# Hybrid decoder trunk: heads' sums and meta part behind the queries, groups' gate and row squares behind bank copies

## The chip, the cores and the metric

The kernel runs on one core of a Trainium2 chip, as one program. The metric is the device time of one execution in microseconds (us). A core has five engines, each with an instruction queue of its own that it works off in order: PE (TensorE, matrix products, which land in PSUM banks), DVE (VectorE), ACT (ScalarE), POOL (GpSimd) and SP (SyncE, which here only issues DMAs). They wait for one another through semaphores. An instruction that waits holds up everything behind it in its own queue.

## The reference

One layer of a decoder: four groups of a short gated convolution and four heads of retention (linear attention with decay) run side by side on the same normalised input, one projection goes in and one out, and a normalisation ends it. Sixteen learned "meta" rows precede the 2048 rows of the sequence.

```python
def reference(x, meta, norm1_g, w_in, conv_w, ret_norm_g, w_out, final_g):
    h = jnp.concatenate([meta_b, x], axis=1)          # 16 + 2048 rows of 1024
    hn = rms_norm(h, norm_g)
    cx, cb, cc, cg, q, k, v, rg = jnp.split(hn @ w_in, 8, axis=-1)   # 8 x 512
    conv_out = cb * conv3(cc * cx, conv_w) * silu(cg)  # causal, 3 taps, per channel
    qf, kf = rotary(q) * 128**-0.5, rotary(k)          # 4 heads of 128
    ret = head_group_norm(retention_chunkwise(qf, kf, v))   # chunks of 128, running state
    mixed = jnp.concatenate([conv_out, ret * silu(rg)], axis=-1)
    h = h + mixed @ w_out
    return rms_norm(h, final_g)[:, N_META:]
```

## The kernel before

**Rounds and units.** The sequence is worked in two rounds (`r`) of 1024 columns. A round has eight units: units 0 to 3 are heads, 4 to 7 convolution groups. `UNITS` gives their order: 4, 0, 1, 2, 3, 5, 6, 7 in the first round and 0 to 7 in the second. In the first round unit 4 is worked by `group_plain`, all other groups by `conv_group`, the heads by `head`. The output projection follows (`output`).

**Quads.** A unit makes two products of 256 x 1024 weights with 1024 x 1024 activations. Each is a `quad`: a Strassen-Winograd scheme of seven block products, numbered 0 to 6 here, into three PSUM banks. Every float32 factor is split in a high and a low part, rounded to fp32r (`split`: ACT writes the high part, DVE the low one), and one block product is 12 matmuls of 128 x 512: four slices times low-by-high, high-by-low, high-by-high. A head's first quad makes keys and values, its second queries and gate; a group's first quad makes the two factors of the convolution's input, its second gate and outer factor.

**Between the products.** `quad` has ACT copy a bank after products 0, 2 and 3 (`copy`, tile `tc`), because later products add into the same bank: product 2 needs the copy after 0, product 4 the one after 2, product 5 the one after 3. After products 0 and 2 it takes a step of a caller's list (`step`; its ACT instructions are kept behind the copy). `take(i, j, ...)` is called with a finished block, after products 1, 4, 5 and 6; mostly DVE reads the bank and the copy there.

**Weights.** `stationary` loads four raw blocks (`ra`), has POOL make four sums of them (`sa` and, in place, `ra`) and splits seven matrices into `wh` (ACT, line 104) and `wl` (DVE, line 116), with three buffers each. They are used in the order of the products; the fourth comes from `sa`.

**Sums.** The Winograd scheme needs four sums of the activations' blocks too. For the second round and for the output they are made ahead: `prepare` is a generator; each `next(later, None)` loads four blocks (`x` or `w`), forms four sums on DVE (lines 177 and 116, with one ACT scaling at line 180 for `x`) and stores them in DRAM (`sums_x`, `sums_w`). `MAKES_SUMS` names the units that take one such step each, at their end.

**Meta.** In the first round each unit multiplies the 16 meta rows by its first weights (`meta_products`, line 412, while the unit before it ends). `meta_state` then loads a rotary table (`mr`), adds and rotates on 16 partitions of DVE (tile `mk`; lines 423 to 437), lets PE form the head's first state (line 439) and ACT copy it. `meta_carry` does the like for a group.

**Row factors.** `row_factors` is a generator for the root mean square of the rows of the next round. Eight steps load 128 rows each and let ACT square and add them (`row_squares`, two instructions on `n` and their accumulator reads); for each half of the round `spread_factors` forms the factors (DVE, POOL's power at line 293) and `spread` puts them on all partitions (DVE line 300, PE line 307, ACT lines 310 and 312).

**Order of the work.** A scheduler lists the instructions of each engine from the order in which the code states them and its own idea of times. `tc.issue_after(i)` keeps the instructions of a block that go to the engine of `i` behind `i`; those for other engines it leaves free.

Of the kernel before, what the change touches and what calls it, by code (L numbers as in the profile page):

```python
# [8 lines left out]
F32 = mybir.dt.float32  # L9
# [4 lines left out]
ALU = mybir.AluOpType  # L14
# [23 lines left out]

MAKES_SUMS = (0, 1, 2, 5), (0, 1, 2, 4)

# [33 lines left out]
def hybrid_trunk(ctx: ExitStack, tc: tile.TileContext, t, out: bass.AP, chunk_decay):  # L74
# [132 lines left out]

    copied = [None]

    def quad(w, m, take, steps=()):  # L210
# [35 lines left out]
        product(3, zb, True)  # L246
        c = copy(zb)
        product(4, xb, False)
        take(1, 1, xb, c)
# [109 lines left out]
    def row_factors(r, f):  # L359

        f.extend([row_tile("rr", r), row_tile("rr2", r), []])
        for j in range(2):
            ss = small.tile([P, 2, CH], F32, name="ss", tag="ss")
            for c in range(CH):
                row_squares(ss, r, j, c)
                yield
            f[2].append(spread_factors(ss, *(a[:, j * HB : (j + 1) * HB] for a in f[:2])))
        yield

# [56 lines left out]

    def meta_state(h, scratch):

        rot = sb.tile([P, HB], F32, name="mr", tag="tc", bufs=COPIES)[:NMETA, : 2 * P].rearrange("p (a c) -> p a c", a=2)
        nc.sync.dma_start(rot, t["rot_m"][h])  # L430
        k, v, a, b = meta_sums(scratch)
# [97 lines left out]

    def conv_group(g, r, m, f, blocks, ahead):  # L530

# [20 lines left out]
        blocks, meta = blocks  # L552
        quad(stationary(blocks), m, take)
        catch_up(0)
        if meta:
            meta_carry(g, meta)
        carry(u, g, r)
        cs = [taps(u[j], g) for j in range(2)]

        def take(i, j, pp, c):  # L560
            if i == 0:
                add(nc.vector, c, pp, c)
                mul(nc.vector, c, c, rr[j])
                nc.scalar.activation(c, c, AF.Silu)  # L564
                mul(nc.gpsimd, cs[j], cs[j], rr[j])
                mul(nc.gpsimd, cs[j], cs[j], c)
                return
            if c is not None:
                add(nc.vector, c, pp, c)
                pp = c  # L570
            mul(nc.vector, cs[j], pp, cs[j])

        n = 2 * (NG + g) + 1
        quad(stationary(load_raw(w_loads(n))), m, take)
        catch_up(1)
# [46 lines left out]

    def head(h, r, m, rot_t, f, turning, blocks, ahead, first=(), between=()):


        between = iter(between)
        to_cross = []
        k, v, late = [None, None], [None, None], []
        tables = [rot_t[:, :, j * HB : (j + 1) * HB] for j in range(2)]

# [28 lines left out]
        def take(i, j, pp, c):  # L659
            d = gen("qg")[:, :HB]  # L660
            if i == 0:
                if c is None:
                    nc.scalar.copy(out=d, in_=pp)
                else:
                    add(nc.vector, d, pp, c)
                rotary(d, tables[j])
                q[j] = d
            else:
# [20 lines left out]
        with tc.issue_after(copied[0].ins):  # L689
            join(1)  # L690
        next(between, lambda: None)()
        if blocks[1]:
            meta_state(h, blocks[1])
        blocks = ahead()
# [159 lines left out]
    for r in range(NR):  # L854
# [43 lines left out]
        else:  # L898
# [6 lines left out]
            later = prepare(load_w_out, sums_w)  # L905
        steps = row_factors(r + 1, factors[r + 1]) if r < NR - 1 else iter(())
        units = UNITS[r]
        turning = None
        special = (first, between)
        for n, unit in enumerate(units):  # L910
# [5 lines left out]
            elif unit < NG:  # L916
                if turning is None:
                    turning = [row_tile(name, 1 - r) for name in ("apart", "across")]
                blocks = head(unit, r, m, rot_t, f, turning, blocks, rest, *(special if unit == 0 else ()))
# [12 lines left out]
            if unit in MAKES_SUMS[r]:  # L932
                next(later, None)

# [43 lines left out]
```

## Time and profile before

| | |
|---|---|
| median of 3 runs | 885.62 us (884.61 to 886.62) |
| profiled execution | 885.25 us, its span 883.4 us |
| granted TensorE clock | 1.00 |
| PE busy | 866.2 us, 98% of the span |
| DVE, ACT, POOL busy | 715.5, 472.1, 397.8 us |

The page's share of busy time says that PE is hardly ever idle, but matmuls are pipelined, and a matmul counts as busy for 0.39 us while one starts every 0.23 us. Idle time of PE between two matmuls is therefore some 0.16 us less than what the second one starts late. Of the stages, which are read from the times of their instructions:

| us of the span | stage | PE idle, us |
|---|---|---|
| 62 to 122 | end of unit 4, unit 0 | 3.8 |
| 122 to 170 | unit 1 | 0.0 |
| 170 to 218 | unit 2, first products of unit 3 | 0.9 |
| 218 to 268 | unit 3 | 0.0 |
| 268 to 302 | unit 5 | 2.0 |
| 302 to 412 | units 6, 7, start of the second round | 0.0 |
| 412 to 566 | heads of the second round | 0.0 |
| 566 to 612 | unit 4 of the second round | 0.9 |
| 612 to 870 | units 5 to 7, output | 0.2 |

Each number of the last column is the length of the window less PE's busy time in it.

### The profile page before, as it was taken

The numbers are of one execution on the slowest core, as the hardware profiler recorded it, in microseconds if no ns is written. First come the engines' busy times: TensorE is split into PE (matmuls) and PEld (weight loads), VectorE is DVE, ScalarE is ACT, GpSimd is POOL, SyncE is SP. The second block draws the span as 40 slices with busy tenths as digits, with TensorE's granted clock in tenths as the row PEclk, the third lists the DMA queues.
The fourth block names the chain that finished last, engine by engine and source line by source line (L and its number), as shares of the span: only waits on it lengthen the run. The fifth ranks groups of instructions, "written<-read, shape, count | busy, mean of one in ns | idle before, by whom it ended". The sixth has DMA issues, their size and how long they took to land.

```text
span 883.4 us, 12729 instructions
## 1 busy us (share of the span) xinstructions
PE 866.2 (98%) x4279; PEld 711.1 (80%) x4279; DVE 715.5 (81%) x1176; ACT 472.1 (53%) x871; POOL 397.8 (45%) x291
## 2 busy tenths in 40 slices
PE   8999899999999999999999999999999999999996
PEld 5778787878888777888888888887888888788885
DVE  6888898979877866899989898787768699666764
ACT  8665437364655564746464645534334475545553
POOL 0554232314135554452233323254547455777873
PEclk9999999999999999999999999999999999999999
DMA  9713444343435552846345353346121493545432
GB/s 340 238 61 73 121 108 132 108 128 123 103 109 186 153 155 71 281 137 187 123 101 162 87 165 84 119 132 191 61 72 60 143 369 108 180 156 190 155 122 81
DMA packets 110033, 125.31 MB, mean 142 GB/s; under 512 B 41424, under 2 KB 58128, under 8 KB 109968
## 3 DMA queue, kind: packets, MB, share of 16 engines
q1 hardware_dynamic: 109968, 124.50, 45.6%
q8 instruction: 34, 0.56, 0.3%
q14 instruction: 31, 0.25, 0.1%
HBM read 90.92 MB, written 25.17 MB: 131 GB/s over the span
## 4 chain that ended last, share of the span: by engine, by line
PE 78%; DVE 11%; DMA 4%; issue 2%; ACT 2%; POOL 1%; SPq 1%; POOLq 0%; DVEq 0%; ACTq 0%
PE pj L221 64%; PE pj L277 7%; DVE wl L116 2%; PE ms L732 2%; PE ms L733 2%; PE ms L722 1%; DVE ml L116 1%; DMA w<-in_w_out 1%; PE ms L709 1%; DVE rot L588 1%; DMA mr<-in_rot_m 1%; DVE rot L587 1%; PE ms L412 1%; PE ms L700 1%; DVE x L177 1%
## 5 line engine op out<-in xcount | busy, mean ns | idle before, releaser
L221 PE MATMUL pj<-mh,wl 128*128 128x512 f32 x1008 | 398.5, 395 | 4.7 <-DVE wl L116 2.1
L221 PE MATMUL pj<-mh,wh 128*128 128x512 f32 x1008 | 393.1, 390 | 0.0
L221 PE MATMUL pj<-ml,wh 128*128 128x512 f32 x1008 | 392.9, 390 | 0.0
L104 ACT CAST wh<-ra 128x512 fp32r<-128x512 f32 x216 | 133.6, 619 | 257.4 <-PE pj L221 218.2
L221 PEld LDWEIGHTS pj<-mh,wl 128*128 128x128 f32 x1008 | 189.3, 188 | 48.6 <-ACT tc L228 3.6
L221 PEld LDWEIGHTS pj<-mh,wh 128*128 128x128 f32 x1008 | 189.2, 188 | 39.8
L221 PEld LDWEIGHTS pj<-ml,wh 128*128 128x128 f32 x1008 | 189.4, 188 | 38.1 <-issue 0.5
L116 DVE TENSOR_TENSOR wl<-ra,wh 128x512 fp32r<-128x512 f32 x216 | 184.6, 856 | 42.4 <-ACT wh L104 42.0
L116 POOL TENSOR_TENSOR ra<-ra 128x512 f32<-128x512 f32 x72 | 113.8, 1580 | 93.7 <-PE ms L412 58.1
L116 POOL TENSOR_TENSOR ra<-sa,ra 128x512 f32<-128x512 f32 x36 | 52.5, 1459 | 99.5 <-DVE wl L116 97.8
L113 POOL TENSOR_TENSOR sa<-ra 128x512 f32<-128x512 f32 x36 | 53.8, 1493 | 92.1 <-DMA ra<-in_w_in 32.4
L228 ACT COPY tc<-pj 128x512 f32<-128x512 f32 x108 | 62.5, 579 | 0.0
L277 PE MATMUL pj<-ml,mh 128*128 128x512 f32 x128 | 50.2, 393 | 0.1
L277 PE MATMUL pj<-mh,mh 128*128 128x512 f32 x128 | 49.9, 392 | 0.0
L277 PE MATMUL pj<-mh,ml 128*128 128x512 f32 x128 | 48.9, 399 | 0.1
L745 POOL TENSOR_TENSOR rp<-rs,neg_half 128x4 f32<-128x4 f32 x16 | 17.8, 1112 | 54.2 <-DVE rs L113 54.1
L537 POOL TENSOR_TENSOR c<-c,rr 128x512 f32<-128x512 f32 x14 | 27.6, 1968 | 24.3 <-DVE c L537 13.0
L795 DVE TENSOR_TENSOR yo<-pj,yo 128x512 f32<-128x512 f32 x32 | 21.9, 686 | 18.7 <-POOL yo L113 13.4
L797 ACT ACTIVATE rot<-yo 128x512 f32<-128x512 f32 x32 | 20.2, 630 | 31.1 <-DVE yo L795 30.7
L537 POOL TENSOR_TENSOR c<-c,tc 128x512 f32<-128x512 f32 x14 | 26.7, 1905 | 19.6 <-ACT tc L564 19.6
L800 POOL TENSOR_TENSOR z<-yo,final_g 128x512 f32<-128x512 f32 x16 | 26.9, 1681 | 16.5 <-DVE yo L795 16.5
L104 ACT CAST wh<-sa 128x512 fp32r<-128x512 f32 x36 | 22.1, 615 | 21.1 <-PE pj L221 21.0
(138 smaller groups left out, 1189.1 us busy)
## 6 DMA issues: line engine op xcount, KB each, us to landing
ra<-in_w_in SPq DMA_DIRECT2D x128, 256.0 KB, 2.8
x<-in_xT SPq DMA_DIRECT2D x48, 256.0 KB, 4.5
w<-in_w_out SPq DMA_DIRECT2D x32, 256.0 KB, 4.7
ra<-mixed SPq DMA_DIRECT2D x32, 256.0 KB, 3.0
yo<-in_x SPq DMA_DIRECT2D x32, 256.0 KB, 4.6
ra<-in_x SPq DMA_DIRECT2D x16, 256.0 KB, 3.2
mixed<-c SPq DMA_DIRECT2D x16, 256.0 KB, 2.7
sums_x<-x SPq DMA_DIRECT2D x16, 256.0 KB, 3.0
```

The lines of the kernel that those rows point to most:

```text
L104: nc.scalar.copy(out=hi, in_=src)
L113: eng.tensor_tensor(out=out, in0=a, in1=b, op=ALU.add)
L116: eng.tensor_tensor(out=out, in0=a, in1=b, op=ALU.subtract)
L221: nc.tensor.matmul(bank, a[:, ks], b, start=first and kt == 0 and n == 0, stop=kt == KH - 1 and n == 2, skip_group_check=not first,)
L228: copied[0] = nc.scalar.copy(out=c, in_=bank)
L277: nc.tensor.matmul(banks[i], a[:, ks], b, start=half + kt + n == 0, stop=half == 1 and kt == KH - 1 and n == 2,)
L537: eng.tensor_tensor(out=out, in0=a, in1=b, op=ALU.mult)
L732: nc.tensor.matmul(o[:, cs], pm[:, cs], vt[j][:, cs], start=True, stop=False)
L745: nc.gpsimd.tensor_tensor(out=rp, in0=rs, in1=neg_half.rearrange("p (c a) -> p c a", a=1), op=ALU.pow)
L795: last[0] = nc.vector.tensor_tensor(out=y, in0=pp, in1=y, op=ALU.add)
L797: nc.scalar.activation(junk, y, AF.Square, accum_out=ss[:, i, j : j + 1])
L800: nc.gpsimd.tensor_tensor(out=ys[i][j], in0=y, in1=final_g[:, j * HB : (j + 1) * HB], op=ALU.mult)
```

## The change

Four things are moved; no arithmetic is added or removed.

- **Heads' sums.** The units that take a step of `prepare` are 1, 2, 3, 5 and 1, 2, 3, 4 in the rounds, where they were 0, 1, 2, 5 and 0, 1, 2, 4. A head takes it right after its second quad, with DVE's part behind the rotation of the first half of the queries; a group with DVE's part behind its last multiplication.
- **Heads' meta part.** The table `mr` has a buffer of its own and is loaded at the head's start. All of the meta part's DVE work stands behind the rotation of the first queries.
- **Groups' gate.** The gate function of the first half (ACT's Silu, POOL's two multiplications) is stated after the copy behind product 2, not inside `take`. `quad` takes a third step, after the copy behind product 3.
- **Row squares.** The ten steps of `row_factors` (eight squares, two spreads) go one by one behind bank copies of units 6 and 7, five in each, where they were taken four at a time after units 5, 6 and 7.

```diff
-MAKES_SUMS = (0, 1, 2, 5), (0, 1, 2, 4)
+MAKES_SUMS = (1, 2, 3, 5), (1, 2, 3, 4)
+
+FACTOR_STEPS = {6: ((0, 0), (0, 1), (0, 2), (1, 0), (1, 2)), 7: ((0, 0), (0, 1), (0, 2), (1, 0), (1, 2))}
...
         zb = ps_proj()
         product(3, zb, True)
         c = copy(zb)
+        step()
         product(4, xb, False)
...
             f[2].append(spread_factors(ss, *(a[:, j * HB : (j + 1) * HB] for a in f[:2])))
-        yield
+            yield
...
-    def meta_state(h, scratch):
-
-        rot = sb.tile([P, HB], F32, name="mr", tag="tc", bufs=COPIES)[:NMETA, : 2 * P].rearrange("p (a c) -> p a c", a=2)
+    def meta_table(h):
+        rot = sb.tile([P, 2, P], F32, name="mr", tag="mr", bufs=1)[:NMETA]
         nc.sync.dma_start(rot, t["rot_m"][h])
+        return rot
+
+    def meta_state(h, scratch, rot):
...
-    def conv_group(g, r, m, f, blocks, ahead):
+    def conv_group(g, r, m, f, blocks, ahead, steps=()):
+        def go_on():
+            next(factors_ahead[0], None)
+
+        def behind(quad, *own):
+            return [lambda n=n: (own[n](), go_on() if (quad, n) in steps else None) for n in range(3)]
...
-        quad(stationary(blocks), m, take)
+        quad(stationary(blocks), m, take, behind(0, idle, idle, idle))
...
+        def gated():
+            j, c = gates.pop()
+            nc.scalar.activation(c, c, AF.Silu)
+            mul(nc.gpsimd, cs[j], cs[j], rr[j])
+            mul(nc.gpsimd, cs[j], cs[j], c)
 
         def take(i, j, pp, c):
             if i == 0:
                 add(nc.vector, c, pp, c)
                 mul(nc.vector, c, c, rr[j])
-                nc.scalar.activation(c, c, AF.Silu)
-                mul(nc.gpsimd, cs[j], cs[j], rr[j])
-                mul(nc.gpsimd, cs[j], cs[j], c)
+                gates.append((j, c))
+                if j == 1:
+                    gated()
                 return
...
-        quad(stationary(load_raw(w_loads(n))), m, take)
+        quad(stationary(load_raw(w_loads(n))), m, take, behind(1, idle, gated, idle))
...
+        with tc.issue_after(queried[0].ins):
+            next(sums, None)
         if blocks[1]:
-            meta_state(h, blocks[1])
+            with tc.issue_after(queried[0].ins):
+                meta_state(h, blocks[1], rot)
...
-                blocks = conv_group(unit - NG, r, m, f, blocks, rest)
-                for _ in range(4 - r):
-                    next(steps, None)
-            if unit in MAKES_SUMS[r]:
-                next(later, None)
+                blocks = conv_group(unit - NG, r, m, f, blocks, rest, FACTOR_STEPS.get(unit, ()) if r == 0 else ())
+                if unit in MAKES_SUMS[r]:
+                    with tc.issue_after(taken[0].ins):
+                        next(later, None)
```

What the scheduler makes of it is shown at three places, engine by engine; line numbers of the changed kernel are some 2 to 29 higher for the same code.

**First place: the meta part of unit 0, second quad.** DVE before, from the third of the four instructions that rotate the first half of the queries (line 589, `qg`) on; `mk` is the meta scratch, `mr` the table, `wl` a weight's low part:

```order
L589 TENSOR_TENSOR qg<-qg,rot_t 128x512
L116 TENSOR_TENSOR wl<-ra,wh 128x512
L590 TENSOR_TENSOR qg<-qg,rot 128x512
L435 TENSOR_TENSOR mk<-mk,mr 16x64 x2
L116 TENSOR_TENSOR wl<-ra,wh 128x512
L436 TENSOR_TENSOR mk<-mk,mr 16x128
L113 TENSOR_TENSOR mk<-mk 16x128
L113 TENSOR_TENSOR qg<-pj,tc 128x512
```

DVE of the changed kernel, from the same instruction on:

```order
L612 TENSOR_TENSOR qg<-qg,rot_t 128x512
L118 TENSOR_TENSOR wl<-ra,wh 128x512
L613 TENSOR_TENSOR qg<-qg,rot 128x512
L115 TENSOR_TENSOR mk<-mk 16x128 x2
L442 TENSOR_TENSOR mk<-mk,mr 16x128
L441 TENSOR_TENSOR mk<-mk,mr 16x64 x2
L115 TENSOR_TENSOR mk<-mk 16x128
L118 TENSOR_TENSOR wl<-ra,wh 128x512
L115 TENSOR_TENSOR qg<-pj,tc 128x512
```

The two first additions (16x128 x2), which stood much earlier, have joined the others, and one `wl` has gone behind them. PE before, at the end of product 5 (`mh_252`) and the start of product 6 (`mh_319`); `ms<-mk` makes the first state, `ra,meta_s` are the next unit's meta products:

```order
L221 MATMUL pj<-ml_253,wh 128x512
L221 MATMUL pj<-mh_252,wh 128x512
L439 MATMUL ms<-mk 128x128
L412 MATMUL ms<-ra,meta_s 16x128 x8
L221 MATMUL pj<-mh_319,wl 128x512
```

PE of the changed kernel, at the end of product 4 (`mh_695`) and the start of product 5 (`mh_234`):

```order
L223 MATMUL pj<-ml_696,wh 128x512
L223 MATMUL pj<-mh_695,wh 128x512
L445 MATMUL ms<-mk 128x128
L415 MATMUL ms<-ra,meta_s 16x128 x12
L223 MATMUL pj<-mh_234,wl 128x512
```

The state's product stands one block product (12 matmuls) earlier than before, and so in all four heads of the first round. The meta products, 8 here and 8 after product 6 before, are now 12 here and 4 after product 5.

**Second place: DVE after unit 0's second quad.** Before, from the last rotation of the queries on; `c<-c,cb` belongs to unit 4, `x` are the sums, `kv` is unit 1's first key block:

```order
L590 TENSOR_TENSOR qg<-qg,rot 128x512
L487 TENSOR_TENSOR c<-c,cb 128x512 x2
L113 TENSOR_TENSOR mk<-mk 16x128 x2
L487 TENSOR_TENSOR c<-c,cb 128x512 x2
L177 SCALAR_TENSOR_TENSOR x<-x,gain 128x512
L116 TENSOR_TENSOR wl<-ra,wh 128x512
L177 SCALAR_TENSOR_TENSOR x<-x,gain 128x512
L116 TENSOR_TENSOR wl<-sa,wh 128x512
L113 TENSOR_TENSOR kv<-pj,tc 128x512
L177 SCALAR_TENSOR_TENSOR x<-x,gain 128x512
L116 TENSOR_TENSOR x<-x 128x512
L116 TENSOR_TENSOR wl<-ra,wh 128x512
```

DVE of the changed kernel at the same place:

```order
L613 TENSOR_TENSOR qg<-qg,rot 128x512
L493 TENSOR_TENSOR c<-c,cb 128x512 x2
L118 TENSOR_TENSOR wl<-ra,wh 128x512
L493 TENSOR_TENSOR c<-c,cb 128x512 x2
L118 TENSOR_TENSOR wl<-sa,wh 128x512
L115 TENSOR_TENSOR kv<-pj,tc 128x512
L118 TENSOR_TENSOR wl<-ra,wh 128x512
```

The four `x` and the two `mk` are gone from here, and the first `wl` has moved ahead of two of unit 4's multiplications.

**Third place: ACT in unit 5's second quad.** Before, from the convolution's first tap (`c<-u,conv_w`) on; `n,ss<-n` is a row square, `tc<-pj` a bank copy, `tc<-tc` the gate function, `x<-x,gain` the sums' scaling:

```order
L472 ACTIVATE c<-u,conv_w 128x512 x2
L336 ACTIVATE n,ss<-n 128x512
L104 CAST wh<-sa 128x512
L228 COPY tc<-pj 128x512
L336 ACTIVATE n,ss<-n 128x512 x3
L104 CAST wh<-ra 128x512
L336 ACTIVATE n,ss<-n 128x512
L755 COPY apart<-pm 128x1024
L336 ACTIVATE n,ss<-n 128x512 x3
L564 ACTIVATE tc<-tc 128x512
L180 ACTIVATE x<-x,gain 128x512
L104 CAST wh<-ra 128x512
```

ACT of the changed kernel, from the same tap on:

```order
L478 ACTIVATE c<-u,conv_w 128x512 x2
L182 ACTIVATE x<-x,gain 128x512
L106 CAST wh<-sa 128x512
L230 COPY tc<-pj 128x512
L106 CAST wh<-ra 128x512
L784 COPY apart<-pm 128x1024
L106 CAST wh<-ra 128x512
L230 COPY tc<-pj 128x512
L579 ACTIVATE tc<-tc 128x512
L106 CAST wh<-ra 128x512
```

The eight squares have left; the scaling of the sums' first block stands ahead of the copy after product 0, and the gate function behind the copy after product 2.

More of the change, by code (lines that the diff above doesn't have):

```diff
@@ L206, in prepared @@
                 parts(m, SUMS[n], kt, a)
-    copied = [None]
+    copied, taken, factors_ahead = [None], [None], [iter(())]
     def quad(w, m, take, steps=()):
@@ L528, in group_plain, with idle @@
         return blocks, (complete, close)
-    def conv_group(g, r, m, f, blocks, ahead):
+    def conv_group(g, r, m, f, blocks, ahead, steps=()):
+        def idle():
+            pass
+        def go_on():
+            next(factors_ahead[0], None)
+        def behind(quad, *own):
+            return [lambda n=n: (own[n](), go_on() if (quad, n) in steps else None) for n in range(3)]
         u = [gen("u") for _ in range(2)]
@@ L558, in conv_group @@
         cs = [taps(u[j], g) for j in range(2)]
+        gates = []
+        def gated():
[3 more added lines that the diff above has]
+            mul(nc.gpsimd, cs[j], cs[j], c)
         def take(i, j, pp, c):
@@ L570, in take @@
                 pp = c
-            mul(nc.vector, cs[j], pp, cs[j])
+            taken[0] = nc.vector.tensor_tensor(out=cs[j], in0=pp, in1=cs[j], op=ALU.mult)
         n = 2 * (NG + g) + 1
-        quad(stationary(load_raw(w_loads(n))), m, take)
+        quad(stationary(load_raw(w_loads(n))), m, take, behind(1, idle, gated, idle))
         catch_up(1)
@@ L621, in catch_up, with head @@
                     waiting[stage].pop(0)()
-    def head(h, r, m, rot_t, f, turning, blocks, ahead, first=(), between=()):
+    def head(h, r, m, rot_t, f, turning, blocks, ahead, sums, first=(), between=()):
         between = iter(between)
-        to_cross = []
+        to_cross, queried = [], []
         k, v, late = [None, None], [None, None], []
+        rot = meta_table(h) if blocks[1] else None
         tables = [rot_t[:, :, j * HB : (j + 1) * HB] for j in range(2)]
@@ L666, in take @@
                 rotary(d, tables[j])
+                queried.append(turned[0])
                 q[j] = d
@@ L905, in hybrid_trunk @@
             later = prepare(load_w_out, sums_w)
-        steps = row_factors(r + 1, factors[r + 1]) if r < NR - 1 else iter(())
+        factors_ahead[0] = row_factors(r + 1, factors[r + 1]) if r < NR - 1 else iter(())
         units = UNITS[r]
@@ L918, in hybrid_trunk @@
                     turning = [row_tile(name, 1 - r) for name in ("apart", "across")]
-                blocks = head(unit, r, m, rot_t, f, turning, blocks, rest, *(special if unit == 0 else ()))
+                sums = later if unit in MAKES_SUMS[r] else iter(())
+                blocks = head(unit, r, m, rot_t, f, turning, blocks, rest, sums, *(special if unit == 0 else ()))
             else:
```

## The prediction

> **What bounds the kernel now.** I read the clock and the page's first part (PE busy 98%, clock 1.00), then the busy time by stages, and then the timeline of PE for single late matmuls. Three of the stages, with the columns PE, PEld, DVE, ACT and POOL busy, each with its count, then clock, DMA share, GB/s:
>
> ```profile
> 218.00:268.00 50.00, 50.00 (x288) 41.96 (x288) 39.19 (x88) 26.13 (x45) 15.42 (x12) 1.00 0.37 100
> 268.00:302.00 34.00, 31.99 (x172) 24.96 (x171) 27.84 (x58) 21.05 (x43) 18.41 (x16) 1.00 0.60 186
> 364.00:412.00 48.00, 47.97 (x213) 39.17 (x212) 47.38 (x62) 32.80 (x57) 20.16 (x10) 1.00 0.61 186
> ```
>
> PE bounds nearly everywhere: in unit 3's stage it never idles, in unit 5's 34.00 - 31.99 = 2.0 us, and where DVE is full, at 364 to 412, 0.03. Only a few places can give time back. PE's timeline names them, with the idle time before the matmul in brackets:
>
> ```profile
> 92.64 0.39 PE L221 MATMUL pj<-mh,wh 128*128 128x512 f32 x1
> 94.12 0.45 PE L439 MATMUL ms<-mk 16*128 16x128 f32 x2 [1.10 <-DVE mk L113]
> 107.24 0.47 PE L221 MATMUL pj<-mh,wl 128*128 128x512 f32 x1 [1.20 <-DVE wl L116]
> 118.47 0.38 PE L732 MATMUL ms<-v,pm 128*128 128x128 f32 x1 [0.98 <-DVE pm L724]
> 216.04 0.38 PE L732 MATMUL ms<-v,pm 128*128 128x128 f32 x1 [0.88 <-DVE pm L724]
> 286.91 0.39 PE L221 MATMUL pj<-mh,wh 128*128 128x512 f32 x1
> 288.73 0.50 PE L221 MATMUL pj<-mh,wl 128*128 128x512 f32 x1 [1.43 <-ACT tc L228]
> 295.09 0.50 PE L221 MATMUL pj<-mh,wl 128*128 128x512 f32 x1 [0.58 <-DVE tc L113]
> 596.36 0.47 PE L221 MATMUL pj<-mh,wl 128*128 128x512 f32 x1 [0.37 <-DVE wl L116]
> 599.88 0.47 PE L221 MATMUL pj<-mh,wl 128*128 128x512 f32 x1 [0.52 <-DVE wl L116]
> ```
>
> Matmuls start 0.23 us apart, so the one at 288.73 is 288.73 - 286.91 - 0.23 = 1.59 us late, 0.16 more than its bracket. I add 0.16 to each: the eight brackets, 7.06 us, stand for 8.3 us. That is all that a change in the order can win here, about 0.9%; the start, the output and the last stores are not touched. In unit 0 the cause is DVE's queue:
>
> ```profile
> 89.49 0.68 DVE L590 TENSOR_TENSOR qg<-qg,rot 128x512 f32<-128x512 f32 x1
> 92.51 0.35 DVE L435 TENSOR_TENSOR mk<-mk,mr 16x64 f32<-16x64 f32 x2 [2.34 <-DMA mr<-in_rot_m]
> 93.39 0.27 DVE L436 TENSOR_TENSOR mk<-mk,mr 16x128 f32<-16x128 f32 x1
> 93.70 0.28 DVE L113 TENSOR_TENSOR mk<-mk 16x128 f32<-16x128 f32 x1
> 100.75 3.48 DVE L487 TENSOR_TENSOR c<-c,cb 128x512 f32<-128x512 f32 x2
> 104.15 0.47 DVE L113 TENSOR_TENSOR mk<-mk 16x128 f32<-16x128 f32 x2
> 104.55 1.27 DVE L487 TENSOR_TENSOR c<-c,cb 128x512 f32<-128x512 f32 x2
> 105.76 0.73 DVE L177 SCALAR_TENSOR_TENSOR x<-x,gain 128x512 f32<-128x512 f32 x1
> 106.42 0.67 DVE L116 TENSOR_TENSOR wl<-ra,wh 128x512 fp32r<-128x512 f32 x1
> ```
>
> DVE stands still 2.34 us for the table `mr`, and the low part that PE waits for at 107.24 is made at 106.42, behind `mk` and one `x`.
>
> **The change part by part.**
>
> *Unit 0, sums gone and `wl` forward.* Ahead of the `wl` at 106.42 the changed queue no longer has the two `mk` (0.47), the last two multiplications (1.27) and the `x` (0.73), nor the 2.34 of idle time earlier; that is over 2 us against a lateness of 1.20 + 0.16 = 1.36 us. Gain 1.36. Behind it two more `x` and their difference are missing too, some 2 us, so `pm` at 118.47 is on time: gain 0.98 + 0.16 = 1.14.
>
> *Meta part, unit 0.* The state's product now stands before product 5. Its DVE chain starts when the rotation ends, 89.49 + 0.68 = 90.17, and takes 0.47 + 0.27 + 0.35 + 0.28 = 1.37: 91.54, and 0.14 later (93.98 to 94.12 before) PE starts, at 91.68. When PE gets there is seen here and in unit 2:
>
> ```profile
> 89.92 0.39 PE L221 MATMUL pj<-mh,wh 128*128 128x512 f32 x1
> 186.47 0.68 DVE L590 TENSOR_TENSOR qg<-qg,rot 128x512 f32<-128x512 f32 x1
> 190.13 0.39 PE L221 MATMUL pj<-mh,wh 128*128 128x512 f32 x1
> 191.28 0.35 DVE L435 TENSOR_TENSOR mk<-mk,mr 16x64 f32<-16x64 f32 x2 [4.14 <-DMA mr<-in_rot_m]
> 192.85 0.39 PE L221 MATMUL pj<-mh,wh 128*128 128x512 f32 x1
> 193.16 0.48 PE L439 MATMUL ms<-mk 16*128 16x128 f32 x2
> ```
>
> Undisturbed, the product starts 0.31 us after the last matmul (192.85 to 193.16). In unit 0 PE is ready at 89.92 + 0.31 = 90.23 and waits 1.45 us; before it waited 94.12 - 92.95 = 1.17. So the first wait of the list does not go, it moves: loss 0.28. In unit 2 the chain is ready at 187.15 + 1.51 = 188.66 and PE at 190.44, 1.8 us of room; units 1 and 3 are laid out alike, and I cost them at nothing. If DVE were over 1.8 us later there, each would pay.
>
> *Unit 2.* DVE loses its 4.14 us wait, and the sums stay. The values that its later work needs come from PE, so not all of the 4.14 comes through; the lateness is 0.88 + 0.16 = 1.04 and I count it as gone. Who is late next: nobody within a microsecond.
>
> *Sums at new places.* Unit 3 gets four `x` steps, at most 4 x 0.73 = 2.9 us, in a stage with 50.0 - 39.2 = 10.8 us of DVE idle: nothing. In the second round unit 4's sums move to the unit's end and unit 0's to unit 3. What they cost at unit 4 now:
>
> ```profile
> 593.34 1.18 DVE L116 TENSOR_TENSOR w<-w 128x512 f32<-128x512 f32 x1
> 596.74 1.28 DVE L116 TENSOR_TENSOR w<-w 128x512 f32<-128x512 f32 x2
> ```
>
> They stand directly before the two late `wl`; without them both are on time: gain (0.37 + 0.16) + (0.52 + 0.16) = 1.21. At the unit's end the next quad's products hide them.
>
> *Row squares, unit 5.* Eight squares and their wait sit ahead of the bank copy that PE waits for at 288.73:
>
> ```profile
> 278.73 0.63 ACT L336 ACTIVATE n<-n 128x512 f32<-128x512 f32 x1 [2.67 <-DMA n<-in_x]
> 286.99 0.71 ACT L180 ACTIVATE x<-x,gain 128x512 f32<-128x512 f32 x1
> 288.11 0.57 ACT L228 COPY tc<-pj 128x512 f32<-128x512 f32 x1
> 288.39 1.77 DVE L300 TENSOR_TENSOR rot<-ident,rc 128x512 f32<-128x512 f32 x1
> ```
>
> They leave: gain 1.59, and with the spread and `x` gone from DVE too the 0.58 + 0.16 = 0.74 at 295.09. Against it, ACT now scales the sums' `x` before the first bank copy. Its transfer takes the place of the squares' in SP's queue:
>
> ```profile
> 274.82 4.38 SPq L335 DMA_DIRECT2D n<-in_x  x8
> x<-in_xT SPq DMA_DIRECT2D x48, 256.0 KB, 4.5
> ```
>
> Issued at 274.8, landed by 278.7 (as `n` did) to 279.3 (4.5 us median), scaled by 280.0; then `wh` (0.6) and the copy (0.57) end at 281.2, while product 2 would be due near 280.1. Loss 0 to 1.2, I take 0.6, the middle, since the transfer may land either side.
>
> *Row squares and spreads, units 6 and 7.* The same instructions, one pair behind a copy. Each copy has a product (12 x 0.23 = 2.7 us) to spare before PE adds into its bank, and a pair takes about 2 x 0.63: nothing, if the rows have landed. The second spread moves into the stage 364 to 412, where DVE is full (47.38 of 48). It adds 0.7 to 1.77 us (the row at 288.39) and some 0.6 of small ones, 2.4 at most; yet PE idles only 0.03 us there, so DVE works ahead. Bounds 0 and 2.4; I take 0.5, near the lower end, because the spread's product delays PE as well.
>
> *Cuts in PE's row of matmuls.* A cut for meta products alone costs:
>
> ```profile
> 283.63 0.39 PE L221 MATMUL pj<-mh,wh 128*128 128x512 f32 x1
> 283.94 0.41 PE L412 MATMUL ms<-ra,meta_s 128*16 128x128 f32 x8
> 284.29 0.50 PE L221 MATMUL pj<-mh,wl 128*128 128x512 f32 x1
> ```
>
> 284.29 - 283.63 - 0.23 = 0.43 us. Unit 6 has two more cuts than before, with the same products in them: 0 to 0.86, I take 0.5. The heads get one more each but shorter ones: nothing, at most 4 x 0.43 = 1.7.
>
> *Gate.* The same Silu and multiplications, later by one copy. POOL's results are needed two products later: nothing.
>
> *Sum.* Gains 1.36 + 1.14 + 1.04 + 1.21 + 1.59 + 0.74 = 7.1; losses 0.28 + 0.6 + 0.5 + 0.5 = 1.9. Net -5.2 us. The profiled execution, 885.25 (span 883.4 and 1.85 around it), becomes 880.05; the median of the runs is 0.37 higher, so 880.4.
>
> **A row and a rule.** POOL's next weights wait for the meta products:
>
> ```profile
> 98.78 1.50 POOL L116 TENSOR_TENSOR ra<-ra 128x512 f32<-128x512 f32 x1 [11.78 <-PE ms L412]
> ```
>
> While POOL runs three such steps, from 98.78 on, two of DVE's multiplications take 3.48 us; the two behind them take 1.27. With the last meta products one block product earlier, POOL's steps come 2.7 us earlier, onto the second rotation. I expect 2.2 us lost as before, at another place. The Trainium skill, "SBUF — State Buffer", Who interferes with whom, states that a VectorE instruction with two SBUF inputs and a GpSimd instruction that reads SBUF exclude each other for the whole instruction; by that rule, with which these durations agree, the sum stays -5.2 as long as the rotations have 2.2 us of room, and is that of the first rival if not.
>
> **The rivals.** *Part is given back (882.0 to 883.85).* POOL's steps block the rotations, and with them `pm`, in units 0 and 2: 2.2 us, the two gains of 1.14 and 1.04, stay lost, and the sum is -3.0: 882.6. For it: 3.48 against 1.27 above. Against it: DVE has lost 2 to 4 us of waiting in both units.
>
> *No change (883.85 to 887.4).* PE waits for the meta state in all four heads as in unit 0, three more times 1.45 = 4.4 us: -0.8, 884.8. For it: the product stands 2.7 us earlier everywhere. Against it: 1.8 us of room in unit 2. Within 0.2%, 1.8 us, a measurement of this kernel can hardly tell a change from none.
>
> *Slower.* ACT's queue waits for rows at eight places. Each pair of squares stands between a bank copy and the next high part; the first square of all waited 2.67 us for its rows at 278.73, and a late copy there has cost PE 1.59. From 0.65 us a place (8 x 0.65 = 5.2) on, the gain is gone; at 0.9 the result is 7.2 - 5.2 = +2.0: 887.6. For it: some of these loads stand in SP's queue behind stores that wait for DVE. Against it: a copy may be a product late.
>
> **How the numbers follow.** Forecast (878.0 to 882.0) 0.60, part given back 0.20, no change 0.12, slower 0.08. Faster by over 0.2% is the first two, 0.80. The lower end is all gains and no loss, 885.6 - 7.1 = 878.5, and 0.5 for what I cannot see; the upper, 884.2, takes in the first rival and the edge of the second.
>
> **What would show it.** Right: no PE wait at the places of 107, 118, 216, 288, 295, 596 and 600, one of about 1.4 us before the first state product only, no DVE wait for `mr`. Wrong: PE idle time before state products of units 1 to 3, before bank copies in units 5 to 7, or between 364 and 412.

## The result and the profile after

The changed kernel takes 880.9 us (median of 4 runs, 880.03 to 881.39), the kernel before, run beside it, 885.8: a ratio of 0.9945 with a 95% interval of 0.9927 to 0.9962. The forecast was 880.4 us. The profiled execution took 880.67 us, with a span of 878.9 where before it was 883.4, and a clock of 1.00.

The list of PE's waits of the changed kernel, with the sum in us, how often, and the longest:

```profile
PE ms L867 <- ACT warm L861: 2.3, 1, 2.3
PE pj L280 <- DVE ml L118: 1.4, 2, 1.0
PE pj L223 <- ACT tc L230: 1.3, 2, 0.8
PE ms L445 <- DVE mk L115: 1.2, 1, 1.2
PE pj L223 <- DVE wl L118: 0.3, 1, 0.3
```

The first row is the wait before PE's first matmul. `pm` is no longer in the list; the other rows bear names that were there before, but most of them stand at new places. PE's timeline shows these one by one (idle time before the matmul in brackets):

```profile
90.65 0.39 PE L223 MATMUL pj<-mh,wh 128*128 128x512 f32 x1
92.23 0.45 PE L445 MATMUL ms<-mk 16*128 16x128 f32 x2 [1.19 <-DVE mk L115]
106.71 0.48 PE L223 MATMUL pj<-mh,wl 128*128 128x512 f32 x1
307.30 0.50 PE L223 MATMUL pj<-mh,wl 128*128 128x512 f32 x1 [0.59 <-ACT tc L230]
370.00 0.50 PE L280 MATMUL pj<-mh,ml 128*128 128x512 f32 x1 [0.98 <-DVE ml L118]
409.14 0.47 PE L223 MATMUL pj<-mh,wl 128*128 128x512 f32 x1 [0.26 <-DVE wl L118]
```

The matmul that stood at 107.24 with 1.20 us of idle time now stands at 106.71 with none; those of 118, 216, 288, 295, 596 and 600 have none either. The first state product still waits. Three waits are new, at 307, 370 and 409. The stages, with PE, PEld, DVE, ACT and POOL busy, then clock, DMA share and GB/s:

```profile
218.00:268.00 50.00, 50.00 (x284) 41.80 (x283) 41.88 (x90) 27.27 (x47) 14.15 (x12) 1.00 0.47 137
268.00:302.00 34.00, 34.00 (x183) 27.29 (x182) 29.21 (x51) 18.40 (x33) 20.96 (x17) 1.00 0.54 163
302.00:364.00 62.00, 61.41 (x291) 48.71 (x290) 44.56 (x64) 35.16 (x76) 31.76 (x25) 1.00 0.54 175
364.00:412.00 48.00, 46.76 (x208) 37.79 (x207) 47.12 (x63) 32.42 (x58) 16.90 (x9) 1.00 0.58 174
```

Unit 5 has lost its 2.0 us of idle PE, and the next two stages have gained 0.6 and 1.2. VectorE is as full as before in the last one (47.12 of 48), and PE now waits for it there.

Three places, from the timelines of DVE, POOL, ACT and SP. In unit 0, the chain to the state product, then the second rotation beside POOL's steps, then `pm`:

```profile
90.22 0.68 DVE L613 TENSOR_TENSOR qg<-qg,rot 128x512 f32<-128x512 f32 x1
90.82 0.47 DVE L115 TENSOR_TENSOR mk<-mk 16x128 f32<-16x128 f32 x2
91.80 0.28 DVE L115 TENSOR_TENSOR mk<-mk 16x128 f32<-16x128 f32 x1
98.75 1.67 DVE L610 TENSOR_TENSOR rot<-qg,rot_t 64x512 f32<-64x512 f32 x1
100.43 1.70 DVE L611 TENSOR_TENSOR rot<-qg,rot_t 64x512 f32<-64x512 f32 x1
115.66 0.74 DVE L753 SCALAR_TENSOR_TENSOR pm<-ms,cols,causal 128x512 f32<-128x512 f32 x1
98.25 1.62 POOL L118 TENSOR_TENSOR ra<-sa,ra 128x512 f32<-128x512 f32 x1
99.94 1.64 POOL L118 TENSOR_TENSOR ra<-ra 128x512 f32<-128x512 f32 x1
```

The six `mk` operations follow the rotation at once, without a wait for the table, and end at 92.08, when PE has stood ready since 90.65 + 0.31. In unit 5 the sums' scaling and the bank copy behind it, and in unit 6 the squares, the copy behind them, and SP's queue:

```profile
276.15 0.72 ACT L182 ACTIVATE x<-x,gain 128x512 f32<-128x512 f32 x1 [2.86 <-DMA x<-in_xT]
277.29 0.58 ACT L230 COPY tc<-pj 128x512 f32<-128x512 f32 x1
304.83 0.63 ACT L339 ACTIVATE n<-n 128x512 f32<-128x512 f32 x1 [2.37 <-DMA n<-in_x]
306.68 0.58 ACT L230 COPY tc<-pj 128x512 f32<-128x512 f32 x1
298.25 1.79 SPq L195 DMA_DIRECT2D sums_x<-x  x3
300.09 2.25 SPq L338 DMA_DIRECT2D n<-in_x  x4
```

The rows of unit 6 are issued at 300.09, behind three stores of the sums; the first square waits 2.37 us for them, and the second bank's copy, which stands behind the squares, reaches PE late.

### The profile page after: what moved, and what is told of

It is laid out like the page before. It is cut to its first block, busy times and chain, and to the rows that moved or that the text cites. A ratio compares the mean times of both kernels' runs of the same rounds, so it can differ in the third digit from the quotient of the medians.

```text
span 878.9 us, 12726 instructions
## 1 busy us (share of the span) xinstructions
PE 864.9 (98%) x4279; PEld 711.0 (81%) x4279; DVE 721.7 (82%) x1176; ACT 472.1 (54%) x871; POOL 397.3 (45%) x291
## 4 chain that ended last, share of the span: by engine, by line
PE 76%; DVE 9%; issue 3%; DMA 1%; POOL 1%; ACT 1%; SPq 0%; POOLq 0%; DVEq 0%; ACTq 0%
PE pj L223 67%; DVE ml L118 3%; PE ms L761 2%; PE ms L762 2%; PE ms L751 2%; PE ms L738 2%; DVE wl L118 1%; PE pj L280 1%; DVE c L480 1%; PE ms L415 1%; PE ms L729 1%; DVE ml L110 1%; DMA t<-sums_x 1%; DVE rot L611 1%; DMA n<-in_x 1%
## 5 line engine op out<-in xcount | busy, mean ns | idle before, releaser
L118 DVE TENSOR_TENSOR wl<-ra,wh 128x512 fp32r<-128x512 f32 x216 | 190.3, 881 | 41.6 <-ACT wh L106 38.8
L778 DVE TENSOR_SCALAR pm<-ms,mv,rp 128x128 f32<-128x128 f32 x64 | 21.9, 403 | 12.4 <-POOL rp L774 12.3
```

Source lines behind the costliest of these rows:

```text
L118: eng.tensor_tensor(out=out, in0=a, in1=b, op=ALU.subtract)
L778: nc.vector.tensor_scalar(out=y[:, cs], in0=o[:, cs], scalar1=mv[:, c, 0:1], scalar2=rp[:, c, :], op0=ALU.subtract, op1=ALU.mult,)
```

## The experiments: the change taken apart

The first four kernels were timed together, beside a kernel before at 886.39 us.

**Sums alone.** The kernel before with the sums at their new places; meta part, squares and gate as they were.

```diff
-MAKES_SUMS = (0, 1, 2, 5), (0, 1, 2, 4)
+MAKES_SUMS = (1, 2, 3, 5), (1, 2, 3, 4)
...
+        with tc.issue_after(queried[0].ins):
+            next(sums, None)
```

> The kernel before with only the heads' and groups' sums moved (units 1, 2, 3, 5 and 1, 2, 3, 4, behind the first queries' rotation or the last multiplication); meta part, gate and row squares as before. Theory A (each late matmul has a queue of its own, and the part that clears that queue removes it): the waits near 107 us (1.36) and 596 and 600 us (together 1.21) go, the one near 118 us (1.14) goes in whole or part, those near 94, 216, 287 and 294 us stay: 3 to 4 us faster than before, 882 to 883. Rival B (what counts is DVE's standing still for the meta table, 11.2 us over the four heads; the sums are only what then comes late): next to nothing, 885 to 886.

Measured: 883.8 us, ratio 0.9973 (0.9962 to 0.9984), between the two expectations.

**Meta part alone.** The kernel before with the table loaded at the head's start and the meta state held behind the first query.

```diff
+        rot = meta_table(h) if blocks[1] else None
...
+            with tc.issue_after(queried[0].ins):
+                meta_state(h, blocks[1], rot)
```

> The kernel before with only the meta part changed (table in a buffer of its own and loaded at the head's start, its DVE work behind the first queries' rotation); sums, gate and row squares as before. Theory A: DVE's wait for the table goes in all four heads; PE's wait near 216 us (1.04) goes, the one near 107 us (1.36) goes too because DVE arrives 2.3 us earlier, the one before unit 0's state product stays at 1.2 to 1.5, those near 287, 294, 596 and 600 us stay: 2 to 3.3 us faster, 882.5 to 884. Then the gains of this part and of the sums overlap near 107 us and don't add up. Rival B (the table's wait is the whole story): 4 to 5 us faster, 881 to 882.

Measured: 884.8 us, ratio 0.9983 (0.9974 to 0.9992), less gain than either expected.

**Squares alone.** The kernel before with the row squares and spreads behind the bank copies of units 6 and 7.

```diff
-                blocks = conv_group(unit - NG, r, m, f, blocks, rest)
-                for _ in range(4 - r):
-                    next(steps, None)
+                blocks = conv_group(unit - NG, r, m, f, blocks, rest, FACTOR_STEPS.get(unit, ()) if r == 0 else ())
```

> The kernel before with only the row squares and spreads moved (one step behind a bank copy of units 6 and 7); sums, meta part and gate as before. Theory A: the waits near 287 and 294 us (together 2.3) go, and two come instead that the changed kernel shows: a bank copy in unit 6 behind a square that waits for its rows (0.75 late) and the start of the second round's plain products behind DVE (1.15 late, and 0.4 near 409 us): net 0 to 0.8 us faster, 885 to 885.8. Rival C (the new waits come from the sums, which now share these stages, not from the squares): 2 us or more faster, 883.5 or less, and no wait of PE in unit 6 or at the start of the second round.

Measured: 885.5 us, ratio 0.9986 (0.9977 to 0.9995), as theory A had it, though its late copy in unit 6 doesn't come.

**All but the gate.** The changed kernel with the gate function back in the second bank's take.

```diff
-                if j == 1:
-                    gated()
+                gated()
...
-        quad(stationary(load_raw(w_loads(n))), m, take, behind(1, idle, gated, idle))
+        quad(stationary(load_raw(w_loads(n))), m, take, behind(1, idle, idle, idle))
```

> The changed kernel with the gate function of the first half back at its old place in the code (called as soon as its input is taken); all else as changed. Theory A: the same time as the changed kernel, 880.4 to 881.4, since ACT and POOL have a product's time to spare there. Rival D (the gate function ahead of a bank copy holds up PE): PE waits for bank copies in the groups, 1.5 us or more slower than the changed kernel, 882.4 or above.

Measured: 881.5 us, ratio 0.9946 (0.9932 to 0.996); by the time alone no gain of the gate is seen. It was timed once more:

> The changed kernel with the gate function put back into the second bank's take, a second time, since one call can't tell 0.8 us. If the gate's move is worth the 1.5 us that the trace shows at 593 us without it: ratio to before 0.995 to 0.9965. If it is worth nothing, as the prediction had it: 0.994 to 0.9955, as the changed kernel. The trace is expected to show the 1.3 us wait for the copy at 593 us again.

Measured: 882.2 us, ratio 0.9952 (0.9939 to 0.9966): inside both expectations' ranges, so time doesn't decide. The traces do. What each kernel lost at each place, as us by which the matmul's start was late (its start less that of the matmul ahead, less the distance of an undisturbed pair of that kind; below 0.25 left blank). Plain products do without the Winograd scheme; the first unit of the second round and the output begin with them:

| place | before | sums | meta | squares | no gate | after |
|---|---|---|---|---|---|---|
| state product, unit 0 | 1.17 | 1.00 | 1.26 | 1.04 | 1.26 | 1.26 |
| `wl`, unit 0 (107) | 1.44 | 0.76 | | 1.43 | | |
| `pm`, unit 0 (118) | 1.15 | | 2.14 | 1.18 | | |
| `pm`, unit 2 (216) | 1.04 | | | 1.14 | | |
| copy, unit 5 (288) | 1.59 | 1.43 | 1.81 | | | |
| 295 | 0.74 | | 0.79 | | | |
| copy, unit 6 (307) | | | | | 0.99 | 0.75 |
| plain product (370) | | | | 1.24 | 1.24 | 1.15 |
| `wl` at 409 | | | | 0.62 | 0.71 | 0.42 |
| unit 4, second round | 1.21 | 1.49 | 1.21 | 1.25 | 1.50 | |
| plain product, output (710) | | 0.82 | 0.82 | 0.81 | | |
| span | 883.4 | 880.2 | 882.7 | 883.7 | 879.7 | 878.9 |

The profiled execution of the sums alone was the fastest of its twelve (881.97 us), so its span lies below that of its median. Four things follow. First, the two waits of unit 0 together need both moves: with the sums alone the one at 118 goes, but the two `mk` additions still stand ahead of the `wl` at 107, and half its lateness stays; with the meta part alone the one at 107 goes, but the `x` operations still stand ahead of `pm`, which is now 2.14 us late instead of 1.15. From DVE's and PE's timelines, first with the sums alone:

```profile
104.61 0.47 DVE L115 TENSOR_TENSOR mk<-mk 16x128 f32<-16x128 f32 x2
107.04 0.47 PE L223 MATMUL pj<-mh,wl 128*128 128x512 f32 x1 [0.52 <-DVE wl L118]
```

and with the meta part alone:

```profile
110.89 1.75 DVE L118 TENSOR_TENSOR x<-x 128x512 f32<-128x512 f32 x1
118.01 0.49 PE L760 MATMUL ms<-v,pm 128*128 128x128 f32 x2 [1.98 <-DVE pm L752]
```

Second, either of the two moves ends the wait at 216. Third, the squares alone bring the new waits at 370 and 409, and what they win in unit 5 (2.3 us) they mostly give back there (1.9). The wait at 307 is seen only where squares and sums are both moved: there the squares' loads stand on SP directly behind the sums' stores, while with the squares alone those stores go out at 284.63, 17 us ahead of the loads (301.30). The wait at 710 was expected by nobody; it comes up again in the last section.

Fourth, the gate. In unit 4 of the second round, ACT without the gate's move (second run) and PE there:

```profile
592.67 0.63 ACT L579 ACTIVATE tc<-tc 128x512 f32<-128x512 f32 x1 [4.39 <-DVE tc L553]
593.71 0.58 ACT L230 COPY tc<-pj 128x512 f32<-128x512 f32 x1
594.34 0.50 PE L223 MATMUL pj<-mh,wl 128*128 128x512 f32 x1 [1.33 <-ACT tc L230]
```

and ACT of the changed kernel:

```profile
591.00 0.58 ACT L230 COPY tc<-pj 128x512 f32<-128x512 f32 x1
592.81 0.63 ACT L579 ACTIVATE tc<-tc 128x512 f32<-128x512 f32 x1 [1.23 <-DVE tc L553]
```

With the sums away, the list of ACT's instructions has the Silu ahead of the bank copy; the Silu waits 4.39 us for VectorE and the copy with it. The gate's move puts the copy ahead again. All three kernels that have the sums' move without the gate's (sums alone and twice without the gate) lose 1.5 us there, and no kernel that has both loses any. The spans without the gate (879.7 and 880.4) are 0.8 and 1.5 above those with it (878.9 and 879.0).

## The experiments: what is left in the changed kernel

Each of the next kernels adds something to the changed kernel, which was run beside the first three of them:

> The changed kernel once more, beside the three that follow, so that they are read against it on the same chip. Expected: a ratio to the kernel before of 0.9935 to 0.9955 (880 to 881.7 us by a median of 885.8), with the four waits that the trace of the changed kernel shows again at their places: the state product of unit 0 (1.2 us), the second bank's copy of unit 6 (0.6 to 0.9), the plain products of row 1 behind an ml split (1.0 to 1.2) and a wl split at 409 us (0.3 to 0.7).

Measured: 881.3 us, ratio 0.9946 (0.9934 to 0.9959), with the four waits at their places (1.26, 0.58, 1.15 and 0.89 us late).

**State product behind product 5.**

`fed[0]` is the last matmul of product 5.

```diff
...
-        nc.tensor.matmul(up[:, :P], k, v, start=True, stop=True)
+        with tc.issue_after(fed[0].ins):
+            nc.tensor.matmul(up[:, :P], k, v, start=True, stop=True)
```

> The changed kernel with one thing more: the state product of the meta part is issued behind the last matmul of product 5 instead of ahead of it, in all four heads (2.7 us of matmuls later on TensorE; with it the next block's meta products go later). Theory: the state product of unit 0 waits 1.2 us because VectorE ends the six small mk operations 1.4 us after product 4 ends; 2.7 us later nothing waits, so 1.0 to 1.26 us go: ratio to the changed kernel 0.9986 to 0.9989, about 879.7 us where the changed kernel gives 880.9. Rival: the meta products behind it release the raw weights 2.7 us later to GpSimd's steps, and the split of the next block's weights comes late: a new wait on wl or on a copy in units 1 to 3 of 0.3 to 1 us each, 880.5 us or more.

Measured: 879.5 us, ratio to before 0.9928 (0.9915 to 0.994), 1.8 us under the changed kernel's median beside it; span 876.9. PE's timeline, with no idle time before the state product:

```profile
92.20 0.39 PE L223 MATMUL pj<-mh,wh 128*128 128x512 f32 x1
92.52 0.48 PE L448 MATMUL ms<-mk 16*128 16x128 f32 x2
```

The theory holds, and no late split appears in units 1 to 3. The gain by the medians is larger than the 1.26 us of the wait; the intervals are too wide to say whether that is more than chance.

**Rows a step ahead.**

```diff
+        if rows is not None and j * CH + c + 1 < 2 * CH:
+            rows.append(load_rows(r, *divmod(j * CH + c + 1, CH)))
```

> The changed kernel with one thing more: each step of the row squares issues the loads of the next step's two rows first, so that the squares of a step find their rows there. Theory: at 307 us the second bank's copy stands on ScalarE behind a square that waited 2.37 us for its row, whose load stood on SyncE's queue behind the sums' stores; with the row loaded a step ahead that wait of 0.6 to 0.75 us at unit 6 goes and no other square's wait is seen: about 880.2 us where the changed kernel gives 880.9 (ratio to it 0.9991 to 0.9993). Rival: the square itself is not what holds the copy, ScalarE's other work is (two squares, 1.6 us with their accumulator reads, stand ahead of the copy whether or not they wait): then the wait at 307 us stays at 0.4 us or more and the time within 0.2 us of the changed kernel.

Measured: 881.4 us, ratio 0.9951 (0.9936 to 0.9965): no gain, the time that the rival had. The mechanism is nevertheless the theory's: the squares find their rows, and no wait is left at 307, nor at 409. Given back were 0.83 us at 710 and 1.3 us at the plain product at 370, which is 2.48 late instead of 1.15:

```profile
370.06 0.50 PE L280 MATMUL pj<-mh,ml 128*128 128x512 f32 x1 [2.31 <-DVE ml L118]
```

It starts when it did in the changed kernel (370.00), though PE's matmuls ahead of it end 1.27 us sooner (the last one starts at 367.36 instead of 368.63). The order of DVE's instructions changed too: two more `ml` splits (0.67 us each) now stand ahead of the one that this product needs. Neither theory named this.

**Second spread earlier.**

```diff
-FACTOR_STEPS = {6: ((0, 0), (0, 1), (0, 2), (1, 0), (1, 2)), 7: ((0, 0), (0, 1), (0, 2), (1, 0), (1, 2))}
+FACTOR_STEPS = {5: ((1, 0), (1, 2)), 6: ((0, 0), (0, 1), (0, 2), (1, 0), (1, 2)), 7: ((0, 0), (0, 1), (0, 2))}
```

> The changed kernel with another table of places: steps behind copies (1,0) and (1,2) of unit 5, the five of unit 6, and (0,0), (0,1), (0,2) of unit 7, so that the second spread comes behind unit 7's copy (0,2), near 347 us, instead of behind (1,2), near 364 us. Theory: the waits of 1.15 us at 370 us and 0.42 at 409 us come from the second spread's VectorE operations in the stretch 359 to 372 us, which VectorE has no gap in; away from there both go: about 879.3 us where the changed kernel gives 880.9 (ratio to it 0.998 to 0.9986). Rival one: that stretch is full by the splits of row 1 alone, and a wait of 0.8 us or more stays at the plain products: 880.5 us or more. Rival two: the squares in unit 5 bring back the late copy there (0.7 to 1.6 us near 288 us), which takes the gain away: 880.5 to 881.5 us.

Measured: 880.4 us, ratio 0.9935 (0.9923 to 0.9948), 0.9 us under the changed kernel's median. The 1.15 at 370 is gone and 0.39 is left near there; from 292 to 302 PE now loses 0.5 and 0.3 us. What the theory and its second rival foretold is seen, each at its place, but this doesn't show that the spread was the cause: a collision of VectorE with GpSimd left the stretch together with it, as the last of these experiments shows.

**All three.**

> The changed kernel with all three: the state product behind product 5, the rows loaded a step ahead, and the table of places that brings the second spread to unit 7's copy (0,2). Theory: the three work at different places, and what each gave back stood in what another mends: the 0.5 and 0.3 us that the earlier table cost in unit 5 were squares that waited for their rows (now a step ahead), and the 2.5 us that the rows ahead brought at 370 us came from the second spread at 364 us and the order that it gives the plain products (now gone). So 1.26 + 0.6 to 0.75 + 1.15 + 0.4 to 0.9 less than the changed kernel: 877.2 to 878.4 us where the changed kernel gives 881 (ratio to before 0.991 to 0.992). Rival: the spread's work on ScalarE and VectorE in unit 7 or unit 5's squares hold a copy back wherever they are put, loaded ahead or not: no better than the state product alone, 879.5 us (ratio to before 0.9925 to 0.9935).

Measured: 879.1 us, ratio 0.992 (0.9908 to 0.9933), the lowest of the kernels that compute the whole. The ratio lies at the edge of the theory's range, the time above it, and the interval overlaps that of the state product alone, so the added gain isn't shown. The theory was wrong on three counts: the 0.5 and 0.3 us stay (the first is a late `wl`, not a square that waits for rows), a wait of 1.43 us stands at 368.89, and one of 0.82 at 709. Without the rows ahead:

> The same without the rows ahead: the state product behind product 5 and the earlier table. Theory: the gains of the two add (1.26, and the 0.9 that the earlier table gave), and the three waits of 0.3 to 0.5 us at 292, 301 and 307 us stay: 878.2 to 879.2 us where the changed kernel gives 881 (ratio to before 0.9915 to 0.9925), and 0.6 to 1.3 us above the kernel with all three. Rival: the rows ahead do nothing for the time, and the two kernels agree within 0.3 us.

Measured: 880.2 us, ratio 0.9929 (0.9916 to 0.9943), with 0.73 us at 307 and the same 1.43. The rows ahead do take the wait at 307 away; the 1.1 us between the two medians are within the intervals.

**One product of GpSimd left out.** The spread was gone from the stretch, and yet 0.39 us with the earlier spread alone had become 1.43 here, with VectorE's instructions in the same order there. What differs there in the two traces is when GpSimd's product of the gate ran. DVE, POOL and PE, of the earlier spread alone:

```profile
366.09 2.73 DVE L110 SCALAR_TENSOR_TENSOR ml<-x,gain,mh 128x512 fp32r<-128x512 f32 x4
368.09 4.90 POOL L553 TENSOR_TENSOR c<-c,tc 128x512 f32<-128x512 f32 x1 [6.26 <-ACT tc L579]
369.57 0.47 PE L223 MATMUL pj<-mh,wl 128*128 128x512 f32 x1 [0.23 <-DVE wl L118]
```

and of all three:

```profile
364.38 3.77 DVE L110 SCALAR_TENSOR_TENSOR ml<-x,gain,mh 128x512 fp32r<-128x512 f32 x4
366.09 1.51 POOL L566 TENSOR_TENSOR c<-c,tc 128x512 f32<-128x512 f32 x1 [5.97 <-ACT tc L592]
368.89 0.47 PE L223 MATMUL pj<-mh,wl 128*128 128x512 f32 x1 [1.27 <-DVE wl L118]
```

So the next kernel is that of all three with one GpSimd instruction less:

```diff
-            mul(nc.gpsimd, cs[j], cs[j], c)
+            if (r, g, j) != (0, NG - 1, 0):
+                mul(nc.gpsimd, cs[j], cs[j], c)
```

> The kernel with all three, with one instruction left out of the computation: GpSimd's product of the convolution with the gate, for the first bank of unit 7 in the first round (c<-c,tc, which ran from 366.09 to 367.60 us there). Every other engine's instructions are the same and in the same order. Theory: the 1.43 us that TensorE loses before the matmul at 368.65 us are 1.04 us of one collision, in which VectorE's four ml splits take 3.77 us because GpSimd's product runs in their middle, and 0.39 us of a full queue; with the product gone the four splits take 2.7 us, TensorE loses 0.3 to 0.5 us there, and the time falls by about 1 us, to a ratio of 0.9905 to 0.992 to the kernel before. Rival: the splits are late for their high parts, which ScalarE makes in turn with casts and copies, or stand behind VectorE's own earlier work, and GpSimd's product only happens to lie there: they take 3.77 us again, TensorE loses 1.2 us or more at the same place, and the time stays.

Measured: 878.1 us, ratio 0.9911 (0.9894 to 0.9927). DVE and PE without the product:

```profile
365.22 2.73 DVE L110 SCALAR_TENSOR_TENSOR ml<-x,gain,mh 128x512 fp32r<-128x512 f32 x4
368.69 0.47 PE L223 MATMUL pj<-mh,wl 128*128 128x512 f32 x1 [0.22 <-DVE wl L118]
```

The four splits take 2.73 us and PE is 0.39 us late: 1.04 us of the 1.43 were the collision with GpSimd, as the theory had it in numbers, and the rival falls. It is this place in the traces that shows it; the two kernels' intervals overlap, and the wait at 709 is gone here too. The Trainium skill, "SBUF — State Buffer", Who interferes with whom, says that of a VectorE instruction with two SBUF inputs and a GpSimd instruction that reads SBUF one is blocked until the other ends, and that the order of issue decides which. The traces agree that one waits: either the product takes 4.90 us and the splits 2.73, or the product 1.51 and the splits 3.77. They add that the loser can wait for more than one instruction: the 4.90 us of the product, from 368.09 to 372.99, run past six VectorE instructions with two SBUF inputs and end beside the next, which takes one of its inputs from PSUM.

The changed kernel has the same collision, which none of the expectations above names. Its DVE and POOL:

```profile
364.30 3.77 DVE L110 SCALAR_TENSOR_TENSOR ml<-x,gain,mh 128x512 fp32r<-128x512 f32 x4
364.92 1.28 POOL L553 TENSOR_TENSOR c<-c,tc 128x512 f32<-128x512 f32 x1 [2.66 <-ACT tc L579]
```

From there VectorE works without a gap up to the `ml` for which PE waits at 370. An estimate from these rows: without the 1.04 us that the splits lose, the 1.15 at 370 would be some 0.1. With the squares alone and without the gate's move GpSimd's product holds up another VectorE operation of the same stretch (`rc`, 1.28 us instead of 0.15). Every kernel with the late spread has the collision, and of those with the earlier spread only the two that lose 0.39 here are without it. What the spread costs by itself is therefore not shown.

## Why the prediction was right, point by point

The time fell by 4.9 us (0.55% of 885.8), 5.2 were forecast. The same measure of lateness as in the table, summed over all matmuls more than 0.06 us late, is 24.9 us before and 20.3 after: 4.6 less, beside 4.5 us of span. By the prediction's terms:

| term | forecast | measured |
|---|---|---|
| unit 0, `wl` | -1.36 | -1.44 |
| unit 0, `pm` | -1.14 | -1.15 |
| unit 2, `pm` | -1.04 | -1.04 |
| unit 4, second round | -1.21 | -1.21 |
| unit 5, copies, less the scaling | -1.59 - 0.74 + 0.6 | -2.45 |
| state product, unit 0 | +0.28 | +0.09 |
| cuts in units 6 and 7 | +0.5 | -0.4 |
| rows in units 6 and 7 | 0 | +0.75 |
| stage 364 to 412 | +0.5 | +1.57 |
| first 70 us | not named | +1.0 |

The rest is -0.3 in pieces. The first 70 us hold nothing that the change touches, and the second profiled execution of the changed kernel lost only 0.3 more there than the kernel before: rather chance than the change.

- *The seven waits.* All went, to within 0.1 us each in the heads, and unit 3, where the sums went, still has no idle PE (50.00 of 50.00 us). The reading that one microsecond of lateness at PE is worth one microsecond of time held.
- *Unit 5.* The 0.6 for the scaling ahead of the copy was not needed. That its transfer was issued at 272.04 instead of 274.82 is no reason: by then the whole kernel ran 2.8 us earlier (PE's first meta products of this quad at 277.43 instead of 280.21). The copy ended at 277.87, and product 2 started only at 278.21. The sum had it due where product 1 ends, but the meta products stand in between and took some 0.8 us.
- *State product.* It moved rather than went, in unit 0 alone, as forecast; the wait was 1.26 where 1.45 was worked out, since the chain took 1.26 us, not 1.37, and began 0.08 before the rotation's row ends. PE and VectorE both came there 0.7 us later than worked out, which cancels.
- *Stage 364 to 412.* This step was mis-sized: 0.5 was taken near the lower end because PE idled only 0.03 us there, read as VectorE working ahead. It had less slack than was added. The squares alone lose as much there (1.24 + 0.62), so the term belongs to their move. Two things stand in it that no kernel with the late spread separates: the spread's operations, which the prediction named, and the 1.04 us of the collision with GpSimd, which it did not.
- *Cuts.* The charge of 0.5 for meta products did not come. The -0.4 is mostly the spreads' own matmuls, which the prediction did not count here: the second matmul of a spread and one behind the pair were together 0.8 us late twice before, and 0.3 and 0.7 after.
- *Rows.* "Nothing, if the rows have landed" was the wrong branch at one place of eight, that of the rival that ends slower: 0.75 us where it assumed at least 0.65. No copy behind the other seven was late.
- *Gate, "nothing".* This step failed. The credit of 1.21 for unit 4 went to the sums' move, but with the sums' move alone 1.5 us are lost there; it takes the gate's move for the wait to go. The sum was right because the whole was made, the assignment was not.
- *Part given back.* GpSimd's steps did move onto the second rotation and stretched it by 2.0 us (1.67 and 1.70 where such an operation otherwise takes 0.69), and the `wl` ahead of it by 0.9 (1.62, not 0.67): 2.9 against 2.2 forecast. `pm` was still in time, so that rival fell. *No change* fell with the waits list: the state product waits once, not four times.

So errors of both signs met: 1.8 us too little lost at 307 and in the stage from 364, 1.6 too much charged to unit 5 and to cuts. The seven waits were read right; that the total came out within 0.3 us of the sum is in good part luck.

## What to carry to other kernels

Where one engine bounds, list its late instructions one by one and ask for each what stands ahead of its releaser in an in-order queue; here those few rows gave what was won to within 0.2 us at every place in the heads and in unit 4, and the errors lay in what was lost. So ask the same of every queue that the moved work enters: where an engine is busy 47.4 of 48 us, added work is likely to come through, and a load behind stores holds up everything behind its consumer. Parts of one edit can depend on each other through a scheduler's order, so a part that is worth nothing by itself may be what keeps another's gain.

## What had not been expected

A collision between VectorE and GpSimd fell differently in two kernels with the same VectorE order in that stretch, and decided 1.04 us of TensorE's time. The running time of the GpSimd product was 4.90 us when it lost and 1.51 when it won, so a long GpSimd row can mean that VectorE was not held up at all, and a short one that it was. The group's row by source line in the trace of all three shows the cost as a spread, not as a mean (min, median and max in ns):

```profile
L110 DVE SCALAR_TENSOR_TENSOR ml<-x,gain,mh x4: 735/737/1780, 364.4 to 366.4; 128x512 fp32r<-128x512 f32 x4
```

Three of the four splits are undisturbed; one takes 1.04 us more.

The wait near 710 looks like a second such collision. In the eight traces without it GpSimd's `c<-c,rr` of the second round's unit 7 takes 3.55 to 3.56 us, and the VectorE split beside it 1.18 to 1.20; in the six traces that have it (0.81 to 0.83 us late) the product takes 2.34 to 2.95 and the split 1.66 to 1.79. No experiment removes this one, so it stays a reading. If it holds, a change at 300 us can win or lose 0.8 us at 710, and a difference of that size between two kernels need not come from the place that was changed.
